# Scores of the index, B and A heads as float32r products over 128 rows

## The chip, the cores and the metric

The kernel runs on one core of one Trainium2 chip. The metric is the device time of one execution in microseconds (us). The kernel before has a median of 1068.8 us over three runs (1068.74 to 1068.98). Engines are named as in the profile: PE is TensorE's matmuls and PEld its weight loads, DVE is VectorE, ACT ScalarE, POOL GpSimd, SP SyncE, which issues the loads.

## What is computed

Two layers of a decoder trunk for 256 tokens of width 1024, all in float32. Each layer is a half-step SwiGLU block, a mixer, and a second half-step SwiGLU block:

```python
h = h + 0.5 * swiglu(rms_norm(h, ffn1_norm[l]), ...)
h = h + hybrid_mixer(rms_norm(h, mix_norm[l]), w_in[l], ...)
h = h + 0.5 * swiglu(rms_norm(h, ffn2_norm[l]), ...)
```

The mixer projects the normed input to the parts of three head groups:

- Group A, 4 query heads of 64 on one shared key and value head. An indexer with 8 heads of 64 gives each query its keys: `score = sum over heads of w * relu(qi . ki)`, causal, and the best 64 keys are kept. The choice depends on which scores are larger, so the products behind it have to be as exact as float32.
- Group B, 4 heads. With 256 tokens and blocks of 256 it is plain causal attention.
- Group C, 8 heads with a forget gate and an output gate.

A and B normalise and rotate queries and keys; the index rotates them. All outputs go through `w_out`.

## The kernel before, in words

The activations stay in SBUF as `hres`, 128 features on the partitions by 256 tokens. Weights come from HBM in pieces of 1 MB and are split into two float32r parts by class `Weights`: `high` (L117, ACT) copies a unit to `wh`, `low` (L121, DVE) writes `wl = raw - wh`. A product of weights is then three float32r products, high by high, high by low, low by high (`mm3`). `pump` issues one such split ahead of its use; up to seven units are split ahead.

The whole program is in an order written out by hand (`manual_schedule`): each engine executes its instructions in the order in which the program issues them, and waits where one needs data or a buffer.

In `mixer`, the projection has eight chunks of columns (`iq`, `ib`, `b`, `a`, `ck`, `cq`, `cv`, `cg`), each in four steps, so 32 steps. A step is one unit of weights: two blocks of 128 features by two halves of the tokens by three products, so 12 products of up to 512 columns into two PSUM banks of tag `gu`. After each step `pump` splits a unit and `run_side` issues the side work that is due. After the four steps of a chunk its `post_` function evicts the banks (`evac`, L591, ACT) and enters side work with `at_step(n, fn)`. Side work of one step runs in the order in which it was entered. The steps that matter here:

- 8 and 9: `turn` of iq, 10: `turn` of ik. `pairs_T` (L598, L600) transposes two heads at once, 128 tokens by 128 features, on PE, and ACT copies the result to SBUF.
- 9, 13, 17: `bq_norm`, `bk_norm`, `a_norm`: square sums on DVE, a power on POOL (`rsqrt`, L304), and the scaling of the heads on POOL (`scale_heads`, L577). The rotations of B and A (`rope`, L569 to L572) run on POOL, those of the index on POOL and DVE.
- 13: `turn` of bq; `log_sigmoid` on ACT (L655 to L659, with two table loads).
- 11 to 16: `index`. Two groups of four heads for the first 128 tokens (128 keys), then four groups of two heads for the others (256 keys). Each is a bank of products, a ReLU by ACT (L675), and one weighted sum per head on DVE (L679).
- 16 to 23: `topk`, one round in each step on DVE (L698, L700), 24: `amask`. 16: `cumsum`, whose bank DVE evicts (L722, L723).
- 17 (`B_TURN`): `turn` of bk. 18 to 21 (`B_STEP`): scores of the four B heads. 22 (`A_TURN`): `turn` of aq and ak. 25 to 28 (`A_STEP`): scores of the four A heads.
- `run_heads` works a head: `scores` (two products into a bank, DVE adds the mask and takes the maximum, L848; exponentials on ACT, L855 and L856), two steps later `flip` (three transposes, L862, and a copy, L864, by ACT for even heads and DVE for odd ones), a step later `values` (products with v, and L878 and L887 on DVE), and after each second head `outT` (L895 to L903).

Side work writes to PSUM through `bank("acc")`: four banks that are handed out in turn, so that each is used again for the fourth allocation after it, once its readers are done. Scratch tiles in SBUF (`tmp`) go round in the same way over nine buffers.

The index, B and A products are float32 with 64 rows: two heads share a transposed tile, one on partitions 0 to 63 and one on 64 to 127, and keys are doubled so that they lie on both halves:

```python
mm(b[:, 0:P], q[:, 0:P], k[:, 0:P], True, True)
mm(b[:, P:3 * P], q[:, P:S], k[:, 0:S], False, True)
```

All products go through `mm` (L293), which is therefore the line of most PE rows.

Of the kernel before, what the change touches and what calls it, by code (L numbers as in the profile page):

```python
# [10 lines left out]
F32 = mybir.dt.float32  # L11
F32R = mybir.dt.float32r
# [6 lines left out]
P = 128  # L19
# [122 lines left out]
def kernel(ctx: ExitStack, tc: tile.TileContext, x, ffn1_norm, ffn1_w_gate, ffn1_w_up, ffn1_w_down,  # L142
# [17 lines left out]
    def bank(tag):  # L160
        return psum.tile([P, 512], F32, name="ps_" + tag, tag=tag)
# [117 lines left out]
    future = cst[:, 256:384]  # L279
    cs = cst[:, 384:640].rearrange("p (t c) -> p t c", t=2)  # L280
    causal = cp.tile([P, 3 * P], F32, name="causal")
    cqa = [at.tile([P, 8, 66], F32, name=f"cqa{t}", tag=f"cqa{t}") for t in range(2)]
    cka = [at.tile([P, 8, 66], F32, name=f"cka{t}", tag=f"cka{t}") for t in range(2)]
    va = [at.tile([P, 13, 65], F32, name=f"va{t}", tag=f"va{t}") for t in range(2)]
# [262 lines left out]
    def mixer(l, norm, nxt):  # L547
# [45 lines left out]
        def pairs_T(dsts, srcs, tag):  # L593

            ps = bank(tag)
            for i, s2 in enumerate(srcs):
                for t in range(2):
                    T.transpose(ps[:, i * S + t * P:i * S + (t + 1) * P], s2[t], ident)  # L598
            for i, d in enumerate(dsts):
                A.copy(d, ps[:, i * S:(i + 1) * S])  # L600

        st = {}


        def turn(dsts, srcs):

            return lambda: pairs_T(dsts, [[srcs[t][:, j * P:(j + 1) * P] for t in range(2)]
                                          for j in range(len(dsts))], "acc")

        def post_iq(ps):  # L610
            rot = [[hp.tile([P, S], F32, name="iqr", tag="hl") for _ in range(2)] for t in range(2)]
            for t in range(2):
                for jj in range(2):
                    evac(rot[t][jj], ps[t][:, jj * S:(jj + 1) * S], t)
                    rope(heads(rot[t][jj], 4), cs[:, t, 0:64], cs[:, t, 64:128], V)
            st["iqT"] = [hp.tile([P, S], F32, name="iqT", tag="hh") for _ in range(4)]
            for jj in range(2):
                at_step(8 + jj, turn(st["iqT"][2 * jj:2 * jj + 2], [rot[t][jj] for t in range(2)]))

        def post_ib(ps):  # L620
            ss = sm.tile([P, 2, 4], F32, name="ssbq", tag="ss")
# [29 lines left out]
            st["bqT"] = at.tile([P, 2, S], F32, name="bqT", tag="bqT")  # L651
            at_step(13, turn([st["bqT"][:, 0], st["bqT"][:, 1]], rot))

            def log_sigmoid():
                A.activation(la, lf, AF.Abs)  # L655
# [3 lines left out]
                A.activation(la[:, 0, 0:1], ones[:, 0:1], AF.Exp)  # L659

            at_step(13, log_sigmoid)
            st["ikT"] = hp.tile([P, S], F32, name="ikT", tag="hh")
            at_step(10, turn([st["ikT"]], [d.rearrange("p a b -> p (a b)") for d in ikd]))

            def index(t, heads_):
                n = P * (t + 1)
                b = bank("acc")
                par = heads_[0] % 2
                for i, h in enumerate(heads_):
                    sl = slice(64 * par, 64 * par + 64)  # L670
# [4 lines left out]
                A.activation(rl[:, :n4], b[:, :n4], AF.Relu)  # L675
                sc = st["score"][t]
                for i, h in enumerate(heads_):
                    first = h == 0
                    V.scalar_tensor_tensor(sc, rl[:, i * n:(i + 1) * n], st["iw"][:, t, h:h + 1],  # L679
                                           st["cmask"][t] if first else sc, op0=ALU.mult, op1=ALU.add)  # L680
# [6 lines left out]
            n_idx = 11  # L687
            for t in range(2):
                per = 4 // (t + 1)
                for i0 in range(0, 4, per):  # L690
                    for par in range(2):
                        at_step(n_idx, lambda t=t, hs=[2 * i + par for i in range(i0, i0 + per)]: index(t, hs))
                        n_idx += 1

            def topk():
                m8 = [sm.tile([P, 8], F32, name="m8", tag="m8") for t in range(2)]
# [29 lines left out]
        def post_a(ps):  # L726
            ss = sm.tile([P, 2, 5], F32, name="ssa", tag="ss")
            rot = [hp.tile([P, S], F32, name="aqr", tag="hl") for _ in range(2)]
            ak = [at.tile([P, 1, HD], F32, name=f"ak{t}", tag=f"ak{t}") for t in range(2)]
            akd = [at.tile([P, 2, HD], F32, name=f"akd{t}", tag=f"kd{t}") for t in range(2)]  # L730
            sq = []
            for t in range(2):
                evac(rot[t], ps[t][:, :256], t)
                evac(ak[t][:, 0], ps[t][:, 256:320], t)
                evac(va[t][:, 0, 0:64], ps[t][:, 320:384], t)
                sq.append(squares(ps[t][:, :320], t, 5))
                rope(heads(rot[t], 4), tab[:, 0, 0, t], tab[:, 0, 1, t])
# [11 lines left out]
            st["aqT"] = at.tile([P, 2, S], F32, name="aqT", tag="aqT")  # L749
            st["akT"] = at.tile([P, S], F32, name="akT", tag="akT")  # L750
            at_step(A_TURN, turn([st["aqT"][:, 0], st["aqT"][:, 1]], rot))
            at_step(A_TURN, turn([st["akT"]], [d.rearrange("p a b -> p (a b)") for d in akd]))

            def qk_a(h):
                sl = slice(64 * (h % 2), 64 * (h % 2) + 64)
                return st["aqT"][sl, h // 2], st["akT"][sl]

            run_heads([("A", h) for h in range(4)], qk_a, "acc", lambda i, fn: at_step(A_STEP + i, fn), 2)

        def post_b(ps):  # L760
            ss = sm.tile([P, 2, 4], F32, name="ssbk", tag="ss")
            rot = [hp.tile([P, S], F32, name="bkr", tag="hl") for _ in range(2)]
            sq = []
            for t in range(2):
                evac(rot[t], ps[t][:, :256], t)
                evac(va[t][:, 1:5, 0:64], heads(ps[t][:, 256:512], 4), t)
                sq.append(squares(ps[t][:, :256], t, 4))
                rope(heads(rot[t], 4), tab[:, 3, 0, t], tab[:, 3, 1, t])
# [9 lines left out]
            st["bkT"] = at.tile([P, 2, S], F32, name="bkT", tag="bkT")  # L778
            at_step(B_TURN, turn([st["bkT"][:, 0], st["bkT"][:, 1]], rot))

            def qk_b(h):
                sl = slice(64 * (h % 2), 64 * (h % 2) + 64)
                return st["bqT"][sl, h // 2], st["bkT"][sl, h // 2]

            run_heads([("B", h) for h in range(4)], qk_b, "acc", lambda i, fn: at_step(B_STEP + i, fn), 2)

# [204 lines left out]
    def before_mixer(l):  # L991
        if l == 0:
            turn_gains(1)
            turn_gains(2)
            V.memset(causal[:, P:2 * P], 0.0)
# [114 lines left out]
```

## Time and profile before

| | |
|---|---|
| median of 3 runs | 1068.8 us (1068.74 to 1068.98) |
| profiled execution | 1069.04 us |
| its span, first to last instruction | 1067.3 us |
| mean granted TensorE clock | 1.000 |
| mixer of layer 1, its 32 steps | 198.5 to 308 us |
| mixer of layer 2, its 32 steps | 727 to 836.5 us |

The profile is of one execution. A row of a timeline has the start in us from the span's start, the length, the engine, the line in the kernel, the operation, what it writes and reads, and how many instructions were merged. A row of a group has the busy time and the mean length in ns of one instruction, and after a second bar the engine's idle time before them. `128*128 128x512` on a PE row is rows by columns of the weight tile, then the moving operand. A float32 product shows as two PE records, a float32r product and a transpose as one.

### The profile page before, as it was taken

To read this page: it belongs to the slowest core of one execution; us is meant where nothing else is said; L and a number is where in the kernel's file an instruction comes from. 1 tells how busy PE (TensorE), PEld (TensorE's weight loads), DVE (VectorE), ACT (ScalarE), POOL (GpSimd) and SP (SyncE) were. 2 spreads that over 40 slices of the span, in tenths; PEclk is the share of its full clock that TensorE was granted. 3 is DMA by queue.
4 is the path that set the end of the run, shared out by engine and by line. 5 is a ranking of instruction groups with operands and counts; after the bars stand their busy time and mean duration, and the time that the engine had idled before them with its cause. 6 is when DMAs were issued, how large, how long until landed. Compare 5 with 4: busy or idle time off the path is not lost.

```text
span 1067.3 us, 16804 instructions
## 1 busy us (share of the span) xinstructions
PE 1059.1 (99%) x6571; PEld 944.9 (89%) x6571; DVE 820.6 (77%) x1547; ACT 583.6 (55%) x998; POOL 162.0 (15%) x188
## 2 busy tenths in 40 slices
PE   9999999999999999999999999999999999999998
PEld 8999999987889899999989999999877998888887
DVE  5998777779766797777779877777796668977774
ACT  5665554666554565555456555546765455655551
POOL 2004000277400100000010200003865000000000
PEclk9999999999999999999999999999999999999999
DMA  9576464464332365554645565555554313664631
GB/s 323 203 238 205 157 233 151 148 211 157 121 117 80 119 223 178 191 198 158 198 158 184 190 226 167 189 173 176 164 170 141 119 41 121 235 235 150 207 119 39
DMA packets 130911, 181.79 MB, mean 170 GB/s; under 512 B 7008, under 2 KB 104720, under 8 KB 130832
## 3 DMA queue, kind: packets, MB, share of 16 engines
q1 hardware_dynamic: 130512, 180.65, 50.1%
q8 instruction: 51, 0.84, 0.3%
q14 instruction: 28, 0.23, 0.1%
q10 hardware_dynamic: 320, 0.08, 0.0%
HBM read 179.67 MB, written 1.05 MB: 169 GB/s over the span
## 4 chain that ended last, share of the span: by engine, by line
PE 97%; DVE 1%; DMA 1%; ACT 0%; SPq 0%; issue 0%
PE ps_gu L293 64%; PE ps_acc L293 31%; PE ps_gu L962 1%; DVE xhl L320 1%; DMA xin<-in_x_dram 1%; PE ps_acc L862 0%; PE ps_gu L862 0%; PE ps_acc L598 0%; DVE hres L352 0%; ACT xhl L317 0%; PE ps_gu L895 0%; PE ps_acc L383 0%; PE ps_acc L895 0%; DVE tmp L424 0%; ACT rb L349 0%
## 5 line engine op out<-in xcount | busy, mean ns | idle before, releaser
L121 DVE TENSOR_TENSOR wl<-raw,wh 128x1024 fp32r<-128x1024 f32 (+2 forms) x343 | 418.4, 1227 | 20.6 <-ACT wh L117 20.3
L293 PE MATMUL ps_gu<-xhl,wh 128*128 128x512 f32 (+1 forms) x1408 | 352.7, 392 | 3.5 <-DVE tmp L424 2.6
L117 ACT CAST wh<-raw 128x1024 fp32r<-128x1024 f32 (+2 forms) x343 | 345.1, 1034 | 12.3 <-PE ps_gu L293 6.8
L293 PEld LDWEIGHTS ps_gu<-xhl,wh 128*128 128x128 f32 x1408 | 253.6, 189 | 51.6 <-DVE xhl L320 2.9
L293 PEld LDWEIGHTS ps_gu<-xhl,wl 128*128 128x128 f32 x1400 | 191.5, 190 | 13.5
L293 PE MATMUL ps_gu<-xhl,wl 128*128 128x256 f32 x1400 | 197.3, 283 | 0.0
L293 PE MATMUL ps_gu<-wh,xhl 128*128 128x512 f32 (+2 forms) x512 | 163.7, 385 | 0.0
L424 DVE TENSOR_TENSOR tmp<-ps_gu,tmp 128x256 f32<-128x256 f32 x175 | 74.1, 424 | 111.2 <-ACT tmp L423 110.9
L293 PE MATMUL ps_acc<-hl,wh 128*128 128x256 f32 x528 | 149.7, 284 | 0.0
L293 PE MATMUL ps_acc<-hh,wh 128*128 128x256 f32 x528 | 149.4, 283 | 0.0
L293 PE MATMUL ps_acc<-hh,wl 128*128 128x256 f32 x528 | 149.4, 283 | 0.0
L423 ACT COPY tmp<-ps_gu 128x256 f32<-128x256 f32 x175 | 64.7, 370 | 128.6 <-PE ps_gu L293 123.1
L293 PEld LDWEIGHTS ps_gu<-wh,xhl 128*128 128x128 f32 x512 | 94.8, 188 | 22.1 <-issue 7.3
L293 PEld LDWEIGHTS ps_acc<-hl,wh 128*128 128x128 f32 x528 | 101.4, 192 | 0.3
L293 PEld LDWEIGHTS ps_acc<-hh,wl 128*128 128x128 f32 x528 | 101.4, 192 | 0.0
L293 PEld LDWEIGHTS ps_acc<-hh,wh 128*128 128x128 f32 x528 | 101.4, 192 | 0.0
L293 PE MATMUL ps_gu<-wl,xhl 128*128 128x512 f32 (+2 forms) x256 | 95.8, 374 | 0.0
L331 POOL TENSOR_TENSOR ssacc<-ssacc,tmp 128x512 f32<-128x512 f32 x10 | 12.9, 1294 | 509.8 <-ACT tmp L329 329.8
L431 ACT ACTIVATE tmp<-tmp 128x256 f32<-128x256 f32 x88 | 36.8, 418 | 85.2 <-DVE tmp L429 85.2
L440 ACT CAST hh<-tmp 128x256 fp32r<-128x256 f32 x80 | 32.6, 407 | 87.9 <-DVE tmp L436 87.9
L293 PEld LDWEIGHTS ps_gu<-wl,xhl 128*128 128x128 f32 x256 | 48.3, 189 | 6.3
L429 DVE TENSOR_TENSOR tmp<-tmp,rb 128x256 f32<-128x256 f32 x88 | 37.8, 430 | 3.0
(241 smaller groups left out, 1204.2 us busy)
## 6 DMA issues: line engine op xcount, KB each, us to landing
raw<-in_ffn_w_down_dram SPq DMA_DIRECT2D x44, 1024.0 KB, 6.7
raw<-in_ffn_w_gate_dram SPq DMA_DIRECT2D x43, 1024.0 KB, 7.0
raw<-in_ffn_w_up_dram SPq DMA_DIRECT2D x43, 1024.0 KB, 5.2
raw<-in_w_in_dram SPq DMA_DIRECT2D x24, 1024.0 KB, 5.2
raw<-in_w_out_dram SPq DMA_DIRECT2D x8, 1024.0 KB, 4.9
raw<-in_w_in_dram SPq DMA_DIRECT2D x4, 768.0 KB, 4.8
raw<-in_w_in_dram SPq DMA_DIRECT2D x4, 656.0 KB, 4.4
xin<-in_x_dram SPq DMA_DIRECT2D x4, 256.0 KB, 5.2
```

The source lines that it names most:

```text
L117: self.nc.scalar.copy(hv, src)
L121: (engine or self.nc.vector).tensor_tensor(lv, self.srcs[self.n_low], hv.bitcast(F32), op=ALU.subtract)
L293: T.matmul(o, l, r, start=start, stop=stop, skip_group_check=True)
L320: V.scalar_tensor_tensor(self.l[:, m], hres[:, m] if src is None else src, gT[:, self.col + m:self.col + m + 1], self.h[:, m].bitcast(F32) ...
L331: G.tensor_tensor(self.acc, self.acc, sq, op=ALU.add)
L423: A.copy(o, ps[:, 1])
L424: V.tensor_tensor(o, ps[:, 0], o, op=ALU.add)
L429: V.tensor_tensor(t_, t_, norm.rb, op=ALU.mult)
L431: A.activation(th, t_, AF.Tanh, scale=0.5)
L440: (V.tensor_copy if late else A.copy)(hh, t_)
L962: T.transpose(b[:66, i * S + t * P:i * S + (t + 1) * P], src[t][:, 2 * hp_ + i, :], ident)
```

## The change

A float32 value is split into two float32r parts, high and low, as the weights already are. For the index, B and A heads:

- `stack` writes a query head's high part (ACT) and low part (DVE) side by side, 64 and 64 columns, for each half of the tokens. It is new side work: iq at steps 7 and 8, bq at 14, aq at 20.
- `queries_T` turns one head at a time, so that the high part is on partitions 0 to 63 and the low part on 64 to 127. It does so by float32r products with an identity, `identr`, not by transposes. iq turns at steps 9 and 10 (8 and 9 before), bq at 17 (13 before), aq at 22.
- `keys_T` turns keys that are doubled (k, k), one head at a time, and writes two tiles: the high parts (ACT) on all 128 partitions, and the low parts (DVE).
- `products` is then two float32r products over 128 rows: (high, low) of q by high of k, and by low of k, into one sum, in place of one float32 product over 64 rows.
- `bk_norm` scales and doubles bk in one POOL operation of 512 columns for each half of the tokens.
- `index` takes heads in their order, in groups as large as before.

Tiles that stood for themselves now share buffers (`kT` for iq and bk, `qs` for bq and aq, `ikT` for ik and ak). Group C is as before. The core of the diff:

```diff
+        def stack(x):
+            q = tp.tile([P, 512], F32R, name="stacked", tag="tmp").rearrange("p (h s d) -> p h s d", h=4, s=2)
+            x = heads(x, 4)
+            A.copy(q[:, :, 0], x)
+            V.tensor_tensor(q[:, :, 1], x, q[:, :, 0].bitcast(F32), op=ALU.subtract)
+            return q.rearrange("p h s d -> p h (s d)")
+
+        def queries_T(dst, qs):
+            for j in range(2):
+                ps = bank("acc")
+                for i in range(2):
+                    for t in range(2):
+                        mm(ps[:, i * S + t * P:i * S + (t + 1) * P], qs[t][:, 2 * j + i], identr, i + t == 0, True)
+                A.copy(dst[:, 2 * j:2 * j + 2], ps.rearrange("p (h s) -> p h s", h=2))
+
+        def keys_T(dst, ks):
+            n = dst.shape[2]
+            for j in range(0, n, 2):
+                m = min(2, n - j)
+                ps = bank("acc")
+                for i in range(m):
+                    for t in range(2):
+                        T.transpose(ps[:, i * S + t * P:i * S + (t + 1) * P], ks[t][:, j + i], ident)
+                src = ps[:, :m * S].rearrange("p (h s) -> p h s", h=m)
+                A.copy(dst[:, 0, j:j + m], src)
+                V.tensor_tensor(dst[:, 1, j:j + m], src, dst[:, 0, j:j + m].bitcast(F32), op=ALU.subtract)
+
+        def products(o, q, k, start, stop):
+            mm(o, q, k[0], start, False)
+            mm(o, q, k[1], False, stop)
...
             for jj in range(2):
-                at_step(8 + jj, turn(st["iqT"][2 * jj:2 * jj + 2], [rot[t][jj] for t in range(2)]))
+                at_step(7 + jj, lambda jj=jj: split(jj))
+                at_step(9 + jj, lambda jj=jj: turn_iq(jj))
...
-            at_step(13, turn([st["bqT"][:, 0], st["bqT"][:, 1]], rot))
...
+            at_step(14, bq_split)
+            at_step(B_TURN, bq_turn)
...
-                    mm(b[:, i * n:(i + 1) * n], st["iqT"][h // 2][sl, t * P:(t + 1) * P], st["ikT"][sl, :n],
-                       i == 0, i == len(heads_) - 1)
+                    products(b[:, i * n:(i + 1) * n], st["iqT"][:, h // 4, h % 4, t * P:(t + 1) * P],
+                             [st["ikT"][:, c, 0, :n] for c in range(2)], i == 0, i == len(heads_) - 1)
...
-            at_step(A_TURN, turn([st["aqT"][:, 0], st["aqT"][:, 1]], rot))
-            at_step(A_TURN, turn([st["akT"]], [d.rearrange("p a b -> p (a b)") for d in akd]))
+            def a_turn():
...
+                queries_T(st["aqT"], st["aq"])
+                keys_T(st["akT"], [d.rearrange("p a b -> p (a b)")[:, None] for d in akd])
+            at_step(20, a_split)
+            at_step(A_TURN, a_turn)
...
-                    scale_heads(heads(rot[t], 4), heads(rot[t], 4), rs[:, 4 * t:4 * t + 4])
+                    twice = tmp(512).rearrange("p (h s d) -> p h s d", h=4, s=2)
+                    G.tensor_tensor(twice, heads(rot[t], 4)[:, :, None, :].to_broadcast([P, 4, 2, HD]),
+                                    rs[:, 4 * t:4 * t + 4, None, None].to_broadcast([P, 4, 2, HD]), op=ALU.mult)
...
-                mm(b[:, 0:P], q[:, 0:P], k[:, 0:P], True, True)
-                mm(b[:, P:3 * P], q[:, P:S], k[:, 0:S], False, True)
+                if kind == "C":
+                    mm(b[:, 0:P], q[:, 0:P], k[:, 0:P], True, True)
+                    mm(b[:, P:3 * P], q[:, P:S], k[:, 0:S], False, True)
+                else:
+                    products(b[:, 0:P], q[:, 0:P], [c[:, 0:P] for c in k], True, True)
+                    products(b[:, P:3 * P], q[:, P:S], [c[:, 0:S] for c in k], False, True)
```

More of the change, by code (lines that the diff above doesn't have):

```diff
@@ L281 @@
     causal = cp.tile([P, 3 * P], F32, name="causal")
+    identr = cp.tile([P, P], F32R, name="identr")
     cqa = [at.tile([P, 8, 66], F32, name=f"cqa{t}", tag=f"cqa{t}") for t in range(2)]
@@ L615, in post_iq, with split, turn_iq @@
                     rope(heads(rot[t][jj], 4), cs[:, t, 0:64], cs[:, t, 64:128], V)
-            st["iqT"] = [hp.tile([P, S], F32, name="iqT", tag="hh") for _ in range(4)]
+            qs = {}
+            def split(jj):
+                qs[jj] = [stack(rot[t][jj]) for t in range(2)]
+            def turn_iq(jj):
+                if jj == 0:
+                    st["iqT"] = at.tile([P, 2, 4, S], F32R, name="iqT", tag="kT")
+                queries_T(st["iqT"][:, jj], qs[jj])
             for jj in range(2):
-                at_step(8 + jj, turn(st["iqT"][2 * jj:2 * jj + 2], [rot[t][jj] for t in range(2)]))
+                at_step(7 + jj, lambda jj=jj: split(jj))
+                at_step(9 + jj, lambda jj=jj: turn_iq(jj))
         def post_ib(ps):
@@ L650, in post_ib, with bq_split, bq_turn @@
             at_step(9, bq_norm)
-            st["bqT"] = at.tile([P, 2, S], F32, name="bqT", tag="bqT")
-            at_step(13, turn([st["bqT"][:, 0], st["bqT"][:, 1]], rot))
+            def bq_split():
+                st["bq"] = [stack(x) for x in rot]
+            def bq_turn():
+                st["bqT"] = at.tile([P, 4, S], F32R, name="bqT", tag="qs")
+                queries_T(st["bqT"], st["bq"])
+            at_step(14, bq_split)
+            at_step(B_TURN, bq_turn)
             def log_sigmoid():
@@ L661, in post_ib @@
             at_step(13, log_sigmoid)
-            st["ikT"] = hp.tile([P, S], F32, name="ikT", tag="hh")
-            at_step(10, turn([st["ikT"]], [d.rearrange("p a b -> p (a b)") for d in ikd]))
+            st["ikT"] = at.tile([P, 2, 1, S], F32R, name="ikT", tag="ikT")
+            at_step(10, lambda: keys_T(st["ikT"], [d.rearrange("p a b -> p (a b)")[:, None] for d in ikd]))
             def index(t, heads_):
@@ L689, in post_ib @@
                 per = 4 // (t + 1)
[L690 to L693, printed above, removed]
+                for i0 in range(0, 8, per):
+                    at_step(n_idx, lambda t=t, hs=list(range(i0, i0 + per)): index(t, hs))
+                    n_idx += 1
             def topk():
@@ L994, in before_mixer @@
             turn_gains(2)
+            V.tensor_copy(identr, ident)
             V.memset(causal[:, P:2 * P], 0.0)
```

32 lines of the change are left out of this document (12 added, 20 removed).

## The prediction

> **What bounds the kernel now.** The page comes first: busy time of the engines, and the chain that ended last.
>
> ```profile
> PE 1059.1 (99%) x6571; PEld 944.9 (89%) x6571; DVE 820.6 (77%) x1547; ACT 583.6 (55%) x998; POOL 162.0 (15%) x188
> ...
> PE 97%; DVE 1%; DMA 1%; ACT 0%; SPq 0%; issue 0%
> ```
>
> TensorE carries 97% of the chain, so an instruction taken from PE counts in full if nothing else is late. All that changes lies in the two mixers. The view of waits for PEld over the first mixer (198 to 308 us) has this as its longest line:
>
> ```profile
> PEld ps_gu L293 <- issue: 3.7, 11, 0.3
> ```
>
> PE waits for nobody there. But 77% for DVE is a mean, so I cut the mixer into windows (columns: stretch, length, busy PE, PEld, DVE, ACT, POOL):
>
> ```profile
> 240.10:250.50 10.40, 10.40 (x53) 8.41 (x52) 10.19 (x25) 8.58 (x19) 7.75 (x8) 1.00 0.45 133
> 250.50:262.90 12.40, 12.40 (x56) 8.99 (x55) 12.37 (x45) 4.87 (x9) 11.85 (x17) 1.00 0.47 153
> 262.90:270.50 7.60, 7.60 (x47) 6.38 (x46) 7.53 (x27) 6.12 (x12) 0.10 (x1) 1.00 0.36 133
> 277.50:308.00 30.50, 30.50 (x155) 24.21 (x154) 19.01 (x43) 16.34 (x28) 14.70 (x7) 1.00 0.41 136
> ```
>
> From 240.1 to 270.5 us DVE is busy 30.1 of 30.4 us: it is full too, working off a backlog behind a PE that doesn't yet notice. Only after 277.5 does it have air (19.0 of 30.5). The second mixer has the same shape, so I work one out and double it.
>
> **PE's own sum.** Timeline of PE: one index group of four heads with 128 keys, one of two heads with 256, and one B head, each between products of the projection.
>
> ```profile
> 226.40 0.39 PE L293 MATMUL ps_gu<-wh,xhl 128*128 128x512 f32 x1
> 226.71 1.16 PE L293 MATMUL ps_acc<-ikT,iqT 64*128 64x128 f32 x8
> ...
> 228.14 0.39 PE L293 MATMUL ps_gu<-wl,xhl 128*128 128x512 f32 x1
> ...
> 237.65 0.34 PE L293 MATMUL ps_gu<-wh,xhl 128*128 128x384 f32 x1
> 237.92 1.13 PE L293 MATMUL ps_acc<-ikT,iqT 64*128 64x256 f32 x4
> ...
> 239.26 0.34 PE L293 MATMUL ps_gu<-wl,xhl 128*128 128x384 f32 x1
> ...
> 255.78 0.39 PE L293 MATMUL ps_gu<-wh,xhl 128*128 128x512 f32 x1
> 256.09 0.92 PE L293 MATMUL ps_acc<-bkT,bqT 64*128 64x128 f32 x4
> ...
> 257.28 0.39 PE L293 MATMUL ps_gu<-wl,xhl 128*128 128x512 f32 x1
> ```
>
> Each float32 product is two records. Between the named starts lie the group and two projection products (0.17 us each at 384 columns, 0.23 at 512). Without those two the groups cost 228.14-226.40-0.46 = 1.28, 239.26-237.65-0.35 = 1.26 and 257.28-255.78-0.46 = 1.04 us.
>
> What takes their place: two float32r products over 128 rows for each float32 one, as many records as before. Pace of such records, and of a transpose, from the timeline and the groups by form:
>
> ```profile
> 160.44 1.12 PE L293 MATMUL ps_gu<-xhl,wl 128*128 128x256 f32 x8
> 161.39 1.78 PE L293 MATMUL ps_gu<-xhl,wh 128*128 128x512 f32 x7
> ...
> 248.99 0.60 PE L598 MATMUL ps_acc<-cst,bkr 128*128 128x128 f32 x4
> ```
> ```profile
> L293 PE MATMUL ps_gu<-xhl,wh 128*128 128x512 f32 x1392 | 349.9, 393 | 3.5 <-DVE tmp L424 2.6 <-DVE xhl L320 0.9
> L293 PE MATMUL ps_gu<-xhl,wl 128*128 128x256 f32 x1400 | 197.3, 283 | 0.0
> ...
> L598 PE MATMUL ps_acc<-cst,bkr 128*128 128x128 f32 x8 | 1.2, 271 | 0.0
> ```
>
> 256 columns: (1.12-0.28)/7 = 0.12 us; 512 columns: (1.78-0.39)/6 = 0.23. So streaming 128 columns could be done in some 0.06 (below). A transpose, 128 columns with a new weight tile each, takes (0.60-0.27)/3 = 0.11. No row shows float32r at 128 columns; its bounds are 0.06 and the two records of the same float32 shape, 0.22. I take 0.11, that of the transpose, because it too loads 128 weight columns for 128 moving ones.
>
> So a two-head group falls to 4 x 0.12 = 0.48 (0.78 saved, 4 in a layer), a four-head group to 8 x 0.11 = 0.88 (0.40, twice), an A or B head to 0.46 (0.58, eight): 8.6 us a layer. Added are 16 transposes and turning products (iq, bq and aq turn one head at a time, bk is doubled): 16 x 0.11 = 1.8. PE's own sum is 6.8 us saved a layer, 13.6 in all, 1055.4 us if nobody is late.
>
> **What the others must do for it.** Per layer DVE gets eight subtractions of 256 columns (stack), two more for ik and ak, and two of 512 for bk; ACT as many extra copies of query parts and wider evictions; POOL writes bk twice as wide. The weights' splits and SP's loads stay in number and order. Where these fall decides. The rows that anchor it, first DVE's and ACT's timeline, then POOL's with its groups of 512 columns, then PE's products that open steps 18 and 23:
>
> ```profile
> 240.13 0.48 DVE L679 SCALAR_TENSOR_TENSOR score<-tmp,iw,causal 128x256 f32<-128x256 f32 x1 [1.82 <-ACT tmp L675]
> ...
> 241.06 0.74 DVE L585 TENSOR_REDUCE ssbk<-tmp 128x4 f32<-128x256 f32 x2
> ...
> 250.34 0.16 DVE L723 TENSOR_SCALAR cka<-ps_acc 128x8 f32<-128x8 f32 x1
> ...
> 262.89 1.22 DVE L121 TENSOR_TENSOR wl<-raw,wh 128x1024 fp32r<-128x1024 f32 x1
> ...
> 266.61 1.28 DVE L585 TENSOR_REDUCE c_ss<-tmp 128x8 f32<-128x512 f32 x2
> ...
> 270.31 0.29 DVE L887 TENSOR_TENSOR o<-ps_acc,ri 128x128 f32<-128x128 f32 x1
> ```
> ```profile
> 236.59 1.28 ACT L657 ACT_TABLE_LOAD   x1
> ...
> 238.12 1.28 ACT L659 ACT_TABLE_LOAD   x1
> ...
> 239.52 0.58 ACT L675 ACTIVATE tmp<-ps_acc 128x512 f32<-128x512 f32 x1
> ...
> 263.02 0.50 ACT L856 ACTIVATE p<-tmp,nm 128x256 f32<-128x256 f32 x1
> ```
> ```profile
> 244.71 1.69 POOL L577 TENSOR_TENSOR bkr<-bkr,y_bk 128x256 f32<-128x256 f32 x2
> ...
> 262.03 0.61 POOL L577 TENSOR_TENSOR aqr<-aqr,y_a 128x256 f32<-128x256 f32 x1
> ```
> ```profile
> L577 POOL TENSOR_TENSOR cqa<-cqa,y_c 128x512 f32<-128x512 f32 x4 | 6.1, 1535 | 0.0
> L577 POOL TENSOR_TENSOR cka<-cka,y_c 128x512 f32<-128x512 f32 x4 | 4.2, 1047 | 0.2
> ```
> ```profile
> 249.34 0.49 PE L293 MATMUL ps_gu<-wh,xhl 128*128 128x512 f32 x1
> ...
> 270.20 0.48 PE L293 MATMUL ps_gu<-wh,xhl 128*128 128x512 f32 x1
> ```
>
> A DVE operation of 256 columns takes 0.37 (0.74 for two), of 512 columns 0.64.
>
> Up to step 13 the iq, ik and index edits shift PE by under 1 us, and DVE waits for ACT anyway (1.82 us before 240.13): ACT must get through the two table loads of log_sigmoid. They come no sooner in the new kernel: PE reaches them about 0.5 us later (0.9 for eight more turns, less the cheaper index groups), and the bqT copies that stood before them go. So DVE starts again at about 240.1.
>
> **First stall, step 17.** From there DVE runs without a gap. bq_split (step 14) puts 0.74 in front of the eviction of cumsum, which ends at 250.42 now and at 251.2 then. That matters now because of the banks: tag acc has four, in turn. Step 17 takes four of them (two for bq, two for bk) where it took one, and the fourth is the one that cumsum filled, so the last four transposes of bk_turn wait for DVE. PE, without bq's old turn at step 13 and with four cheaper groups, would end step 17 at about 246; bk's first transposes then wait for POOL's two wide products (244.7 + 2 x 1.05 to 1.54, so 246.8 to 247.8), which costs nothing as long as DVE is later. It goes on at 251.2, does four transposes, and starts step 18 at 251.65 where it started at 249.34: 2.3 us late instead of 1 us early. Queued behind the waiting transposes is all of PE.
>
> **Second stall, step 22.** DVE is 0.8 late at cumsum, and 2.1 late after the two subtractions for bk (1.28). Scores of B heads come from PE early enough (2.3 late, less 0.58 a head), so DVE never rests, and ends head 2's at 265.0 (262.9 + 2.1). Then comes a_split at step 20: its copies stand on ACT behind the exponentials of head 2 (0.50 after 263.02, so 265.6 then), so DVE waits about 1 us and does its two subtractions: the split now at 262.89 starts at 266.8, 3.9 late. POOL doesn't decide it: two wide products at 1.05 to 1.54 instead of 1.69 for both make its whole line 0.4 to 1.4 later, so aqr is there (262.6 now) at 263.0 to 264.0, before ACT is. (Nothing, then; up to 1.4 us if ACT were early.)
>
> From 262.89 to the eviction of B head 1's values (ends 270.6) DVE has no gap; it now ends at 274.4. At step 22 a_turn takes three banks instead of two, and the third, for ak, is the one that holds these values. So PE, which has its step done at 269, waits first for head 1's transposed p, and then for that eviction, and starts step 23 at about 274.7 instead of 270.20: 4.5 late. After that DVE has the air of the last window, and the four A heads give 4 x 0.58 = 2.3 back. A layer ends 2.1 to 2.2 late.
>
> **Sum:** 2 x 2.1 = 4.2 us on the profiled execution's 1069.04 (span 1067.3 and 1.7 around it): 1073.2. The median of the runs shown is 1068.8, 0.2 below; I leave that.
>
> **A rule weighed.** Whether waiting costs more than its own length can't be seen in the mixers, since PE doesn't pause there. The start of the kernel shows the same 14 records twice:
>
> ```profile
> 0.99 3.35 PE L293 MATMUL ps_gu<-ones 128*128 128x128 f32 x14 [0.99 <-POOL minus_half L183]
> ...
> 5.60 2.13 PE L293 MATMUL ps_gu<-ones 128*128 128x128 f32 x14
> ```
>
> 3.35 us after rest, 2.13 later. If a stall of about 3 us brought that state back, the next step's twelve products (2.76 us) would take twice as long, 2.8 us more at each of four stalls: 1073.2 + 11 = 1084. The Trainium skill, "TensorE: Matmul & The Clock Gate", Part 1, has this as a rule: after an idle window of about 3.4 us the clock falls to half until it has been busy for as long. By that rule stalls of 2.5 to 3 us lie just under the window. The first rows agree with a slow start.
>
> **Rivals.**
> - Float32r at 128 columns costs as two float32 records, 0.22: the change then doesn't do what it says where N is 128. The 16 turns of iq and the 16 products of the first two index groups delay step 13, and with it ACT, by 32 x 0.11 = 3.5; the A heads give 0.9 less. A layer is 2.1 + 3.5 + 0.9 = 6.5 late: 1082. For it: every float32r row here has 256 columns or more. Against it: from 512 to 256 the pace follows the columns. 0.20.
> - The second stall doesn't come, because DVE's additions hide in gaps smaller than I can see or ACT frees a_split sooner. Then 2.3 late at step 18, less eight heads (4.6), plus 0.4 for aq: 1.9 early, 1065.2. For it: DVE's 0.37 and 0.64 are of other operations, and a stall only shows when the sum of small terms exceeds PE's lead. 0.20.
> - PE's own sum comes through, 1055 to 1061. For it: 97% of the chain. Against it: DVE has 0.3 us free in 30.4. 0.10.
> - The clock falls, 1084: 0.05.
>
> **How the numbers follow.** Two stalls, 1070 to 1077, has 0.45; it is the likeliest, 1073.2. About 0.2% (2.1 us) is what a measurement of this kernel can tell. Faster than 1067: the third rival and most of the second, 0.25. Within: the rest of it and the low edge of the forecast, 0.15. Slower: 0.60. The forecast's own range is 1070 to 1077. The range for 8 in 10 reaches over the second rival to most of the first, 1062 to 1083; it leaves out PE's own sum and some of the two slow cases.
>
> **What would show it.** Right: PE waits near the last keys' transposes of step 17 (released by DVE L723's line) and near ak's of step 22 (released by the values' eviction); DVE over 97% from 240 to 274; B and A heads at about 0.46 on PE; steps 29 to 31 as long as now. Wrong: no PE gap in the mixers (then the time is 1055 to 1061), or products of 128 columns 0.2 apart (then over 1077).

## The result, and the profile after

The kernel after takes 1071.83 us (median of 11 executions, 1071.06 to 1072.82), the kernel before 1068.89 in the same session (11 executions, 1068.74 to 1069.15): a ratio of 1.0027, 95% interval 1.0019 to 1.0034. It is slower by 2.9 us, and 1.4 us below the prediction. The profiled execution took 1071.99 us, with a span of 1070.2.

First the page of the kernel after: busy time, the granted clock in 40 slices, and the chain that ended last.

```profile
PE 1051.7 (98%) x6611; PEld 950.6 (89%) x6611; DVE 831.7 (78%) x1572; ACT 593.0 (55%) x1014; POOL 162.1 (15%) x188
PEclk9999999998999999999999999999989999999999
PE 90%; DVE 4%; ACT 2%; POOL 1%; issue 1%; DMA 1%; SPq 0%; POOLq 0%; ACTq 0%
```

PE is busy for 7.4 us less than before, and yet the time is longer: PE now waits, its share of the chain fell from 97% to 90%, and DVE, which had 1%, has 4%. The clock row has two slices at 8, one in each mixer. In the kernel after, line numbers are higher: `mm` is L294, `stack` L600 and L601, `queries_T`'s copy L611, `keys_T` L621 to L624, the index sums L718, `cumsum`'s eviction L761, the widened scaling of bk L821, `flip` L917 and L919.

The view of waits for PE over the first mixer of the kernel after (198 to 312 us; sum, times, longest) has two lines:

```profile
PE ps_acc L621 <- DVE cka L761: 4.2, 1, 4.2
PE ps_acc L621 <- POOL tmp L821: 0.9, 1, 0.9
```

Both stand before transposes of bk in step 17, the one on DVE as predicted. Here are PE's rows around it:

```profile
245.65 1.00 PE L294 MATMUL ps_acc<-identr,stacked 128*128 128x128 f32 x8
246.61 0.33 PE L621 MATMUL ps_acc<-cst,tmp 128*128 128x128 f32 x1
247.79 0.55 PE L621 MATMUL ps_acc<-cst,tmp 128*128 128x128 f32 x3 [0.85 <-POOL tmp L821]
252.49 1.08 PE L621 MATMUL ps_acc<-cst,tmp 128*128 128x128 f32 x4 [4.16 <-DVE cka L761]
253.23 0.78 PE L294 MATMUL ps_gu<-wh,xhl 128*128 128x512 f32 x1
253.80 0.63 PE L294 MATMUL ps_gu<-wl,xhl 128*128 128x512 f32 x1
254.23 1.05 PE L294 MATMUL ps_gu<-wh,xhl 128*128 128x512 f32 x2
255.08 0.63 PE L294 MATMUL ps_gu<-wl,xhl 128*128 128x512 f32 x1
```

Three banks' worth of side work in step 17 runs, the fourth waits 4.16 us. Behind it step 18 starts at 253.23 instead of 249.34. Its products then come 0.43 us apart (255.08 - 254.23, over two), where 0.23 was the pace. The view by windows shows why, and how full DVE is (columns as in the prediction; the fourth row is the stretch at half clock):

```profile
240.10:250.50 10.40, 7.38 (x44) 6.38 (x42) 10.22 (x16) 9.50 (x20) 8.46 (x6) 1.00 0.32 102
250.50:262.90 12.40, 10.41 (x42) 8.72 (x43) 12.37 (x46) 3.84 (x7) 11.61 (x19) 0.72 0.51 170
262.90:270.50 7.60, 7.60 (x45) 6.62 (x44) 6.23 (x23) 6.40 (x12) 0.00 (x0) 1.00 0.39 139
...
250.82:257.65 6.83, 5.16 (x15) 4.22 (x16) 6.79 (x24) 1.53 (x2) 6.36 (x13) 0.50 0.43 148
```

Before, PE was busy 30.4 of these 30.4 us; now 25.4. DVE has 28.8 (95%), and 22.6 of 22.8 up to 262.9: PE's wait ends when DVE gets there. For 6.83 us the granted clock is 0.50; the second mixer has the same at 779.9.

The starts of the 32 steps, read from PE's timeline (twelve projection products to a step) and taken from the mixer's own start, compare as follows. The mixer itself starts 0.31 us earlier in the span than before.

| start of step | 13 | 17 | 18 | 19 | 22 | 23 | 25 | 29 | 32 |
|---|---|---|---|---|---|---|---|---|---|
| after less before, layer 1, us | +0.56 | -3.01 | +4.20 | +5.74 | +3.91 | +4.28 | +4.32 | +2.01 | +1.92 |
| layer 2, us | +0.74 | -2.84 | +4.37 | +5.17 | +3.37 | +3.74 | +3.76 | +1.45 | +1.36 |

Up to step 17 the change earns its 3 us. Step 17 loses 7.2, step 18 another 1.5, and each of the eight heads gives 0.5 to 0.6 back. What is left, 1.92 + 1.36 - 0.31 = 2.97 us, accounts for the 2.9 us by which the span grew.

### The profile page after: what moved, and what is told of

Same layout as the page of the kernel before. It is cut to its first block, busy times and chain, and to the rows that moved or that the text cites. A ratio compares the mean times of both kernels' runs of the same rounds, so it can differ in the third digit from the quotient of the medians.

```text
span 1070.2 us, 16907 instructions
## 1 busy us (share of the span) xinstructions
PE 1051.7 (98%) x6611; PEld 950.6 (89%) x6611; DVE 831.7 (78%) x1572; ACT 593.0 (55%) x1014; POOL 162.1 (15%) x188
## 4 chain that ended last, share of the span: by engine, by line
PE 90%; DVE 4%; ACT 2%; POOL 1%; issue 1%; DMA 1%; SPq 0%; POOLq 0%; ACTq 0%
PE ps_gu L294 58%; PE ps_acc L294 30%; DVE score L718 1%; PE ps_gu L1017 1%; DVE xhl L321 1%; DVE wl L121 1%; DMA xin<-in_x_dram 1%; PE ps_acc L917 0%; PE ps_gu L917 0%; POOL swapped L570 0%; DVE hres L353 0%; POOL swapped L571 0%; DVE stacked L601 0%; PE ps_acc L621 0%; ACT wh L117 0%
## 5 line engine op out<-in xcount | busy, mean ns | idle before, releaser
L294 PE MATMUL ps_gu<-xhl,wh 128*128 128x512 f32 (+1 forms) x1408 | 352.7, 392 | 3.5 <-DVE tmp L425 2.6
L294 PEld LDWEIGHTS ps_gu<-xhl,wh 128*128 128x128 f32 x1408 | 253.6, 189 | 51.6 <-DVE xhl L321 2.9
L294 PEld LDWEIGHTS ps_gu<-xhl,wl 128*128 128x128 f32 x1400 | 191.5, 190 | 13.5
L294 PE MATMUL ps_gu<-xhl,wl 128*128 128x256 f32 x1400 | 197.3, 283 | 0.0
L294 PE MATMUL ps_gu<-wh,xhl 128*128 128x512 f32 (+2 forms) x512 | 163.0, 385 | 0.0
L294 PE MATMUL ps_acc<-hl,wh 128*128 128x256 f32 x528 | 149.7, 284 | 0.0
L294 PE MATMUL ps_acc<-hh,wl 128*128 128x256 f32 x528 | 149.4, 283 | 0.0
L294 PE MATMUL ps_acc<-hh,wh 128*128 128x256 f32 x528 | 149.4, 283 | 0.0
L294 PEld LDWEIGHTS ps_gu<-wh,xhl 128*128 128x128 f32 x512 | 96.6, 191 | 14.9
L294 PEld LDWEIGHTS ps_acc<-hl,wh 128*128 128x128 f32 x528 | 101.4, 192 | 0.3
L294 PEld LDWEIGHTS ps_acc<-hh,wl 128*128 128x128 f32 x528 | 101.4, 192 | 0.0
L294 PEld LDWEIGHTS ps_acc<-hh,wh 128*128 128x128 f32 x528 | 101.4, 192 | 0.0
L294 PE MATMUL ps_gu<-wl,xhl 128*128 128x512 f32 (+2 forms) x256 | 97.0, 379 | 0.0
L294 PEld LDWEIGHTS ps_gu<-wl,xhl 128*128 128x128 f32 x256 | 49.1, 192 | 6.5
```

Source lines behind the costliest of these rows:

```text
L294: T.matmul(o, l, r, start=start, stop=stop, skip_group_check=True)
```

## The experiments

Three theories stood after this. **A:** the wait for the fourth bank is the cause; without it the gain of PE arrives. **B:** DVE's order is the cause: take that wait away and the next thing that DVE has to do for PE is late. **C:** the fall of the clock is what turns a gain into a loss. Diffs are against the kernel after, except where another is named. The kernel before had a median of 1068.98 beside the first four and 1069.03 beside the last four.

**The cumsum's eviction late.** Side work `cumsum` goes behind bk's turn, so that no bank waits for its eviction.

```diff
-            at_step(16, cumsum)
+            at_step(23, cumsum)
```

> The changed kernel with one edit: cumsum is entered at step 23 instead of 16, so that no bank of bk_turn waits for its eviction. Theory A (the loss is that one PSUM bank and the clock drop that its stall brings on): the stall of 4.4 us at step 17 and the half clock behind it (about 2.5 us) both go, some 7 us a layer, 1057 to 1059 us. Theory B (DVE's order is late anyway): PE is held up again at step 22, by the transposed p of B head 1, which DVE copies at about 269 us of the span; step 23 then starts some 2.9 us sooner a layer and the time is 1065 to 1067 us. A third answer, that the stall is only moved and nothing gained, gives 1071 to 1072 us.

Measured: 1071.14 us (1070.94 to 1072.31), ratio 1.0021 (1.0013 to 1.003). The longest wait of PE over its first mixer:

```profile
PE ps_acc L294 <- DVE bkT L624: 3.5, 1, 3.5
```

The wait at L621 for DVE is gone, step 18 starts 0.50 earlier than before, and then the first B scores wait 3.5 us for the low parts of bk, DVE's next work. DVE's timeline of this kernel shows when it gets to them:

```profile
252.32 1.21 DVE L121 TENSOR_TENSOR wl<-raw,wh 128x1024 fp32r<-128x1024 f32 x1
...
254.63 1.27 DVE L624 TENSOR_TENSOR bkT<-ps_acc,bkT 128x512 fp32r<-128x512 f32 x2
```

The transposes were done at 249, but two rounds of `topk` and a split of weights stood before the subtraction. The stall only moved, as the third answer had it: A fell. The clock dropped here too, for 3.41 us.

**The wait filled with products on zeros.** While PE waits, ten products whose weight tile is all zeros (columns 128 to 255 of `causal`; the moving operand is the table of cosines and sines) keep it busy; they add nothing to the projection's sum. This takes away the clock's fall and not the wait.

```diff
+FILL = 10
...
             for j in range(0, n, 2):
                 m = min(2, n - j)
+                if j:
+                    for _ in range(FILL):
+                        mm(st["ps"][0][:, :S], causal[:, P:2 * P], cst[:, 384:640], False, False)
                 ps = bank("acc")
...
+            st["ps"] = ps
```

> The changed kernel, and PE is given ten float32 products with a zero weight tile of 256 columns (about 4.3 us) into the open projection bank just where it waits at step 17. They add zero to the sum. PE then doesn't pause, the bank still comes free at the same time. If the half clock after the stall costs time of its own, it goes: about 2.6 us in layer 1 and 1.8 in layer 2, 1067 to 1068 us, and the granted clock is 1.000. If PE would have to wait for DVE later anyway, the time stays at 1071 to 1072 us with a clock of 1.000.

Measured: 1070.87 us (1070.27 to 1072.36), ratio 1.0021 (1.0012 to 1.003). PE's rows, and its waits over the first mixer (lines are 1 to 4 higher in this kernel):

```profile
248.44 4.48 PE L295 MATMUL ps_gu<-cst,causal 128*128 128x256 f32 x20
252.77 0.63 PE L625 MATMUL ps_acc<-cst,tmp 128*128 128x128 f32 x4
253.16 0.48 PE L295 MATMUL ps_gu<-wh,xhl 128*128 128x512 f32 x1
...
270.72 0.88 PE L295 MATMUL ps_acc<-va,pT 128*128 128x65 f32 x6 [0.53 <-DVE pT L923]
...
273.23 0.41 PE L625 MATMUL ps_acc<-cst,akd 128*128 128x128 f32 x2 [0.44 <-ACT pT L923]
```

The granted clock of this profile is 1.000 throughout the mixers. Step 18 takes 3.30 us instead of 5.34 (layer 2: 4.60), and the four transposes 0.39 instead of 0.74: that is the clock's price. In layer 1 this kernel is 2.4 us ahead of the kernel after at step 22 and only 1.04 at step 23, since two waits appear in step 22, first for head 1's p, copied by DVE, then for ak's bank. At the end of the mixers 1.1 and 0.3 us remain. The time lies between the two that were expected. So C fell as the main cause: the clock took 2.4 us in layer 1 and 1.6 in layer 2, but more than half of it from time that PE would have waited for DVE in step 22 anyway.

**Four splits of weights later.** No split after steps 15 to 18, two after each of 23 to 26. The split takes ACT as well as DVE off the tight stretch.

```diff
-                W.pump(2 if name == "iq" else 1)
+                W.pump({15: 0, 16: 0, 17: 0, 18: 0, 23: 2, 24: 2, 25: 2, 26: 2}.get(step[0] + 1, 2 if name == "iq" else 1))
```

> The changed kernel, but no weight unit is split after steps 15 to 18 and two are after steps 23 to 26, so DVE has four subtractions of 1.14 us or more less before the B heads. If DVE's order is what holds PE: cumsum's eviction ends about 2.6 us sooner, the stall falls from 4.4 to about 1.8 us, the clock stays up, and PE next waits a little for aq (POOL) at steps 20 to 22; about 5 us a layer, 1060 to 1063 us. If DVE isn't the cause (PE's products or POOL are), 1070 to 1072 us. If the weights come too late with fewer units ahead, slower than 1072 us.

Measured: 1064.2 us (1063.66 to 1064.35), ratio 0.9954 (0.9941 to 0.9966), 1.2 us above the range given for DVE's order. PE's two longest waits over the first mixer:

```profile
PE ps_acc L294 <- ACT pT L919: 1.1, 1, 1.1
PE ps_acc L294 <- DVE bkT L624: 0.9, 1, 0.9
```

Step 18 starts 1.53 us earlier than before instead of 4.20 later, the mixers end 2.43 and 2.23 earlier, and the clock stays at 1.000. Not one instruction of the change is missing; only other work that can wait stands elsewhere. B holds, and the 0.9 for bk's low parts shows that DVE's order still decides in step 18. Since the edit lightens ACT as well, this run alone doesn't tell the two apart; moving DVE's half of the splits alone was not run. For DVE speak the waits in the kernel after and in the first experiment, which end on DVE, and the run with the doubling on ACT below, where ACT gets work, DVE's own instructions get shorter, and the time falls by 2.4 us.

The same edit in the kernel **before** is the control:

> Control: the kernel before with the edit of e3 alone (no split after steps 15 to 18, two after 23 to 26). In before PE waits for nobody in the mixers, so a lighter DVE there should give nothing: 1068.5 to 1069.5 us. If it gives 3 us or more, what e3 showed is a property of the splits and says nothing of the change.

Measured: 1068.93 us (1068.62 to 1069.21), ratio 0.9999 (0.999 to 1.0008). There nobody waited for DVE, so room on DVE brings nothing.

**The index alone.** Only the index is changed; A and B are as in the kernel before, without the widened scaling of bk and without the splits of their queries.

```diff
-            at_step(14, bq_split)
-            at_step(B_TURN, bq_turn)
+            at_step(13, turn([st["bqT"][:, 0], st["bqT"][:, 1]], rot))
...
-                if kind == "C":
+                if True:
                     mm(b[:, 0:P], q[:, 0:P], k[:, 0:P], True, True)
```

> Only the index is changed; A and B heads stay float32 over 64 rows with their turns at the steps of before. Then no step takes more banks than before and nothing new stands on DVE after step 10. PE's own sum for the index: 4 x 0.78 + 2 x 0.40 saved, 8 x 0.11 added, 3.0 us a layer, so 1062.8 us if PE's sum counts in full when nobody is late (range 1061.5 to 1064.5). If DVE's load bounds even there, 1067 to 1069 us.

Measured: 1067.86 us (1067.6 to 1067.98), ratio 0.9989 (0.998 to 0.9998), and not the 1062.8 of PE's own sum. Its waits over the first mixer:

```profile
PE ps_acc L911 <- ACT p L904: 0.5, 1, 0.5
PE ps_acc L601 <- POOL bkr L578: 0.4, 1, 0.4
```

PE is 2.62 us ahead at step 17, near its own sum of 3.0. It meets bk not yet scaled at step 17, and the exponentials of a B head, which come after DVE's maxima, at step 20. Step 18 starts 1.96 earlier, step 21 only 0.95, and the mixers end 0.71 and 0.53 earlier. Even without new load on the others, PE cannot run 2 us ahead of their chain.

**The doubling of bk on ACT.** POOL scales bk in 256 columns as before, and ACT doubles it at step 16. This tells why DVE was later than its added work.

```diff
+                    scale_heads(heads(rot[t], 4), heads(rot[t], 4), rs[:, 4 * t:4 * t + 4])
+
+            def bk_double():
+                for t in range(2):
                     twice = tmp(512).rearrange("p (h s d) -> p h s d", h=4, s=2)
-                    G.tensor_tensor(twice, heads(rot[t], 4)[:, :, None, :].to_broadcast([P, 4, 2, HD]),
-                                    rs[:, 4 * t:4 * t + 4, None, None].to_broadcast([P, 4, 2, HD]), op=ALU.mult)
+                    A.copy(twice, heads(rot[t], 4)[:, :, None, :].to_broadcast([P, 4, 2, HD]))
                     bk.append(twice.rearrange("p h s d -> p h (s d)"))
...
             at_step(13, bk_norm)
+            at_step(16, bk_double)
```

> The changed kernel, but POOL scales bk in 256 columns as before, and ACT doubles it with two copies at step 16. In the changed kernel four weighted sums of the index (L718, 0.48 us alone) took 1.27, 1.15, 0.68 and 0.83 us while POOL wrote bk twice as wide. If POOL's wide operations slow DVE, those sums come down, cumsum's eviction ends 1 to 1.3 us sooner, the first stall is 3.1 to 3.4 us instead of 4.4, and with the clock drop shorter or gone the time is 1068.5 to 1070.5 us. If those sums were long for another reason (waiting for ACT), they stay long, ACT's two copies come on top, and the time is 1072 us or more.

Measured: 1069.44 us (1068.7 to 1070.89), ratio 1.0006 (0.9997 to 1.0015). The rows that matter are those of DVE and POOL between 245 and 250 us. In the kernel after:

```profile
245.57 2.45 DVE L718 SCALAR_TENSOR_TENSOR score<-tmp,iw,score 128x256 f32<-128x256 f32 x2
247.94 1.47 DVE L121 TENSOR_TENSOR wl<-raw,wh 128x1024 fp32r<-128x1024 f32 x1
249.34 1.54 DVE L718 SCALAR_TENSOR_TENSOR score<-tmp,iw,score 128x256 f32<-128x256 f32 x2
...
252.19 0.16 DVE L761 TENSOR_SCALAR cka<-ps_acc 128x8 f32<-128x8 f32 x1
```
```profile
244.51 3.23 POOL L821 TENSOR_TENSOR tmp<-bkr,y_bk 128x512 f32<-128x512 f32 x2
```

and in this one:

```profile
245.60 1.59 DVE L718 SCALAR_TENSOR_TENSOR score<-tmp,iw,score 128x256 f32<-128x256 f32 x2
247.12 1.21 DVE L121 TENSOR_TENSOR wl<-raw,wh 128x1024 fp32r<-128x1024 f32 x1
248.25 1.27 DVE L718 SCALAR_TENSOR_TENSOR score<-tmp,iw,score 128x256 f32<-128x256 f32 x2
...
250.83 0.16 DVE L761 TENSOR_SCALAR cka<-ps_acc 128x8 f32<-128x8 f32 x1
```
```profile
244.54 2.37 POOL L578 TENSOR_TENSOR bkr<-bkr,y_bk 128x256 f32<-128x256 f32 x2
```

DVE begins the same two index sums at the same time and needs 2.45 us beside POOL's wide products, 1.59 beside the narrow ones. The kernel before, with narrow products too, has 1.59, 1.21 and 1.28 for the same three rows. `cumsum`'s last eviction begins at 250.83 instead of 252.19, 1.36 sooner. PE's wait shrinks less, from 4.2 to 3.3 us: it now ends with ACT's first copy of bq at 251.39, since ACT has the doubling in front of it. The clock falls here too, for 3.41 us. The Trainium skill, "SBUF — State Buffer", section "SBUF: two separate sides", says that a DVE operation with two inputs from SBUF and a POOL operation that reads SBUF exclude each other for a whole instruction. The trace agrees: the two sums that the row merges end at 246.84 and 248.02, each 0.28 us after one of POOL's products (246.56 and 247.74).

**Two tuned orders.** The first gives the splits back later, turns bk ahead of bq, and splits aq a step later:

```diff
-                W.pump(2 if name == "iq" else 1)
+                W.pump({15: 0, 16: 0, 17: 0, 18: 0, 29: 2, 30: 2, 31: 2, 32: 2}.get(step[0] + 1, 2 if name == "iq" else 1))
-            at_step(B_TURN, bk_turn)
+            at_step(B_TURN - 0.5, bk_turn)
-            at_step(20, a_split)
+            at_step(21, a_split)
```

> The changed kernel with three edits of order: no split after steps 15 to 18, two after 29 to 32 (e3 gave them back at 23 to 26, and then a copy of ACT was late at step 28 by 1.1 us); bk_turn ahead of bq_turn and of that step's topk, so that bk's subtractions come 1.2 us sooner on DVE (in e3 the first B scores waited 0.9 to 1.2 us for them); a_split at step 21 instead of 20. If DVE's order is the cause, each of these waits goes, 2 to 2.5 us a layer beyond e3: 1059 to 1061 us. If what is left is POOL's line to aq, the first two give 1 us a layer and the rest stays: 1061.5 to 1063. If ACT's or DVE's order isn't what PE waits for, 1064 as in e3.

Measured: 1067.35 us (1065.67 to 1070.41), ratio 0.9983 (0.9972 to 0.9993), a miss: 1059 to 1061 stood for DVE's order, and none of the three answers has 1067. Its two longest waits:

```profile
PE ps_acc L294 <- DVE cka L761: 1.6, 1, 1.6
PE ps_acc L621 <- POOL tmp L821: 0.8, 1, 0.8
```

With bk turned first, it is bq that waits for the bank of `cumsum`, 1.6 us, close to 0.8 for POOL, and the clock fell for 3.41 us. The second order adds what the first experiment had shown, and puts off a fifth split:

```diff
-                W.pump(2 if name == "iq" else 1)
+                W.pump({14: 0, 15: 0, 16: 0, 17: 0, 18: 0, 24: 2, 29: 2, 30: 2, 31: 2, 32: 2}.get(step[0] + 1, 2 if name == "iq" else 1))
-            at_step(16, cumsum)
+            at_step(23, cumsum)
```

> As e7, and cumsum at step 23, and a fifth split put off (none after 14 to 18, two after 24 and 29 to 32). DVE theory: DVE gets another 1.4 us ahead of the B heads, 1058 to 1061 us, at or a little under e7. If the limit is POOL by now, the same as e7 within 0.5 us. If with only two units ahead the weights come late, slower than e7.

Measured: 1061.25 us (1061.15 to 1061.61), ratio 0.9928 (0.9915 to 0.994): faster than both kernels, and just above the 1058 to 1061 that were expected. Its waits, and the first row of its page:

```profile
PE ps_acc L621 <- POOL tmp L821: 0.6, 1, 0.6
PE ps_gu L294 <- DVE cT L1018: 0.6, 1, 0.6
...
PE 1048.2 (99%) x6611; PEld 947.1 (89%) x6611; DVE 828.4 (78%) x1572; ACT 594.2 (56%) x1014; POOL 154.7 (15%) x188
```

No wait for DVE is left in steps 17 to 22. Step 18 starts 1.28 us earlier than before, step 23 2.89, step 32 4.82 (layer 2: 4.31). Of those 9.1 us the median shows 7.8: the L1018 wait stands behind the mixer's 32 steps, where the splits that were put off are made up for. PE's own sum, 1055.4, is not reached: PE's busy time fell by only 10.9 us (1059.1 to 1048.2), where the sum has 13.6, and 7.8 of these show in the time. How much of the rest is POOL's share in step 17 was not tried.

## Why the prediction was right, point by point

The sign and the mechanism of the first stall were right, and the sum of 4.2 us stands beside 2.9. But it came out near by luck: the first stall and a fall of the clock put PE 5.74 us late at step 19 of layer 1, and the second stall, which was to make step 23 start 4.5 us late, didn't come. Of the two stalls that carry the forecast, one happened.

**Pace of float32r at 128 columns: right; PE's own sum: too high.** The value taken was 0.11, with 0.06 and 0.22 as bounds. PE's timeline of the kernel after, an index group of four heads and a B head:

```profile
227.59 1.00 PE L294 MATMUL ps_acc<-ikT,iqT 128*128 128x128 f32 x8
228.43 0.45 PE L294 MATMUL ps_gu<-wh,xhl 128*128 128x512 f32 x1
...
258.11 0.62 PE L294 MATMUL ps_acc<-bkT,bqT 128*128 128x128 f32 x4
258.57 0.39 PE L294 MATMUL ps_gu<-wh,xhl 128*128 128x512 f32 x1
```

From start to start: 0.84 (0.88 predicted) and 0.46 us (0.46). Eight turns of bq take 0.96 (245.65 to 246.61; 0.88). The rival with 0.22 is refuted. But the sum adds 16 transposes and turning products per layer, and there are 20: eight for iq and four each for bq, aq and bk, as the pages' counts show (6611 - 6571 = 40 in two layers). With 20 x 0.11 = 2.2 it is 6.4 us per layer instead of 6.8. The second tuned order, where nothing slows the clock within the mixers, shows 10.9 us less busy time, some 5.4 per layer. PE's gain is real, if smaller; it only isn't what the time follows, not even with the index alone.

**First stall, place and cause right, size wrong.** The step read: bq's split puts 0.74 in front of `cumsum`'s eviction, which ends at 251.2, and step 18 starts at 251.65. The eviction ended at 252.35 (252.19 + 0.16), and step 18 started at 253.23. bq's split did cost what was said (0.76 for both subtractions in DVE's timeline). Missing were 1.4 us by which DVE's own instructions grew beside POOL: 2.45, 1.47 and 1.54 us for what takes 1.59, 1.21 and 1.27 in the run with the doubling on ACT; 0.2 of them were made up, since DVE had started again at 239.94 and not at 240.1. POOL's line was judged only by when it would be ready ("costs nothing, as long as DVE is later"): its wait indeed costs nothing by itself, 0.85 us before a wait for DVE, but the wide products delayed DVE. That run also shows the cause, since POOL's width is what it changes. So the eviction was 1.15 us later than foretold and step 18 was 1.58; of the other 0.43, 0.35 are four transposes at half clock.

**The clock, given 0.05, fell.** Stalls were sized at 2.5 to 3 us, and said to lie just under the rule's idle time; the first was 4.2, and less is enough (last section). It cost 2.4 us in layer 1 (0.35 on the transposes, 2.04 on step 18), as the run with the zero products shows. The rival's time of 1084 is still wrong: it had four falls and a full price, and the runs had two, each paid back for the most part in step 22.

**Second stall: the step failed in its banks.** It said that ak would take the bank of head 1's values and wait for their eviction at 274.4. PE's rows and DVE's in step 22 of the kernel after:

```profile
272.18 0.78 PE L294 MATMUL ps_acc<-va,pT 128*128 128x65 f32 x6
273.04 1.09 PE L294 MATMUL ps_acc<-identr,stacked 128*128 128x128 f32 x8
274.00 0.41 PE L621 MATMUL ps_acc<-cst,akd 128*128 128x128 f32 x2
```
```profile
270.39 0.55 DVE L919 COPY pT<-ps_acc 128x384 f32<-128x384 f32 x1
...
275.10 0.29 DVE L942 TENSOR_TENSOR o<-ps_acc,ri 128x128 f32<-128x128 f32 x1
```

The transposes of ak run at 274.0, over a microsecond before DVE evicts head 1's values, so they use another bank: in the built program that of head 2's p, which ACT releases. The banks are not handed out strictly in turn. The first half of the step, PE waiting for head 1's p, didn't show either, because PE arrived only at 272.18 and DVE had copied it by 270.94. That this wait is real when PE is earlier is shown by the run with the zero products, where it stands with 0.53 and ak's with 0.44. Step 23 started 4.28 and 3.74 us late, beside the 4.5 foretold, but for another reason: the first stall and the clock had brought the 5.74, of which three heads gave back.

**The end: near, but not for the reason given.** Four A heads give 2.3 back (4.32 to 2.01 in layer 1, 3.76 to 1.45 in layer 2), and the mixers end 1.92 and 1.36 late, where 2.1 to 2.2 stood. Steps 29 to 31 are as long as before, as foretold (the starts of steps 29 and 32 are 2.01 and 1.92 late). DVE, said to be over 97% from 240 to 274, is at 95% (32.32 of 33.90 us). That no second stall comes is what the rival at 1065.2 said, with a chance of 0.20, though it gave other reasons than the bank; its time failed because it kept step 18 at 2.3 us late and the clock up.

## What to carry to other kernels

An engine that carries 97% of the chain can have another right behind it: before you count instructions off the bound engine, cut the stage into windows and look at how full the in-order engines are whose results it needs, and by how much it may run ahead of them. If they are full, don't only count what the change adds to them, but also what runs beside them on POOL; and look for work without a near due time (here splits of weights) that stands in the tight stretch, since moving it was worth 7.6 us on the kernel after (medians 1071.83 and 1064.2) and nothing on the kernel before. Where side work shares a few buffers in turn, check which buffer the built program gives, not which one comes next on paper.

## What the runs showed of the hardware

**The clock falls on windows of 3.41 us that are half idle, not only on idle ones.** All falls within the kernels last 3.41 or 6.83 us, and the two in a run lie 529.06 us apart, 155 times 3.413, as if on a fixed grid. The view by windows on that grid (second number: length, third: PE's busy time, with the clock third from the end), first the kernel after, then the one with the cumsum late, then the first tuned order:

```profile
247.41:250.82 3.41, 0.55 (x3) 0.31 (x3) 3.38 (x5) 2.19 (x4) 3.25 (x5) 1.00 0.09 14
250.82:254.23 3.41, 1.74 (x7) 1.58 (x7) 3.41 (x17) 0.62 (x2) 3.25 (x7) 0.50 0.85 296
```
```profile
249.87:253.28 3.41, 2.04 (x10) 1.50 (x8) 3.37 (x9) 1.50 (x3) 3.17 (x6) 1.00 0.66 210
253.28:256.70 3.42, 1.34 (x7) 1.21 (x8) 3.41 (x11) 0.00 (x0) 3.19 (x7) 1.00 0.25 97
256.70:260.11 3.41, 3.41 (x9) 2.63 (x8) 3.39 (x13) 0.56 (x2) 3.25 (x5) 0.50 0.26 35
```
```profile
246.81:250.22 3.41, 1.76 (x15) 1.65 (x16) 3.27 (x15) 1.57 (x3) 3.17 (x7) 1.00 0.14 52
```

A window in which PE was busy 0.55, 1.74, 1.34 or 1.76 us (at most 52%) is followed by one at half clock. (For 0.55 and 1.34 the next row shows it; behind 1.74 the half clock lasts to 257.65, and behind 1.76 it lasts 3.41 us.) One with 2.04 us (60%) is not, nor is any busier one within the kernels. The Trainium skill, "TensorE: Matmul & The Clock Gate", Part 1, speaks of a free-running window of 3.413 us, with which the grid agrees, and of an idle one, which it need not be: 1.65 us without work in one window were enough. So a stall's price depends on how it lies on the grid. Executions of one program, the first tuned order, differ in this way: three executions with a mean clock of 0.998 took 1065.67 to 1066.02 us, four with 0.997 1067.27 to 1067.64, one with 0.994 1070.41. A window at half clock takes about 0.0016 off the mean (1.7 of 1066 us), so an estimate from these numbers is one, two and four such windows, and some 1.5 us for each. In the run with the zero products, four of the 11 executions have 0.998 and took 1072.19 to 1072.36, the others 0.999 or 1.0 and 1070.27 to 1070.9. Products with a weight tile of zeros count as work: with them the clock stayed at 1.000 over the wait.

**DVE and POOL slow each other by whole instructions.** A sum of 256 columns took 0.5 us alone and 1.2 beside POOL's products of 512 columns (2.45 for two). POOL waits too: its first product of 256 columns ended 0.47 us after the split on DVE beside it both in the kernel before (split to 245.18, product to 245.65) and in the run with the doubling on ACT (245.69 and 246.16), though it took 0.94 us in the one and 1.62 in the other.
